# GpSimd copies the mixed queries of every level for the tiled products, and discarded results are stored in 8 bits

## The chip, the cores and the metric

One core of one Trainium2 chip runs the kernel. The metric is the device time of one execution in microseconds (us). TensorE (PE, with its weight loads shown as PEld), VectorE (DVE), ScalarE (ACT), GpSimd (POOL) and SyncE (SP, which issues the DMAs) each work through their own instruction stream in order, and wait for each other by semaphores.

## The reference

One layer over 2048 latent tokens and 256 context tokens of width 1024, all float32. What matters here is the gated linear recurrence of 8 heads with head width 128, run forwards and backwards:

```
q, i, zf, zb = four projections of h          # per head: (tokens, 128)
f = lb + (1 - lb) * sigmoid(z);  k = 1 - f    # one f and one k for each direction
S_t = diag(f_t) S_{t-1} + k_t v_t^T           # a 128 x 128 state
o_t = S_t^T q_t                               # the two directions are added
```

Beside it stand a gated short convolution, an input projection and an output projection, and RMS norms.

## The kernel before, in words

Large projections. All projections are products of f16 high and low parts, three matmuls for each piece (lines 963 to 965), arranged as seven products of half-size blocks instead of eight. They fill TensorE nearly throughout. The 32 scan segments (8 heads times 4 groups of 512 tokens) are threaded between them: `merge_steps` and `run` emit the steps of a segment's chain (`scan_steps`, with the weights of the table `PACE`) between the matmuls of the next projection. A scheduler then sets each engine's final order.

A segment's chain. Inside a segment the products of the recurrence are built up by levels 0 to 6, where level `lev` joins blocks of B = 2^lev tokens. `K` and `Q` (`s.qf`) hold keys and queries of both directions side by side, 2 x 512 columns. At each level DVE multiplies half of the keys by a decay (`level_k`, line 509) and half of the queries (`level_q`, line 516), in place. For a level, the half of the tokens that takes the forward copy and the half that takes the backward copy are interleaved in runs of B; `mix` is the access pattern that walks them so.

Tiled products. `levels(lev)`, called for levels 0, 2 and 4, issues two sets of sixteen 32 x 32 products (line 656). The trace has two records for each float32 matmul, so one set is 32 records. The first set (`i` = 0) uses the tiles that were kept: `ks` and `q` for level 0, `km` and `qm` of level 1 or 3 later. The second set (`i` = 1) uses `km` of the level itself, copied by ACT into one piece (`mixed`, line 626), and the queries, read through `mix` out of `Q`. `held(lev)`, for levels 1, 3 and 5, has GpSimd copy the mixed queries into the tile `qm` (line 633, one buffer) before `level_q` overwrites `Q`. `level6` uses `qm` of level 5 (line 675), then `K` and `Q` directly (line 682).

So within a segment the order on the queries is: `Q` made (line 592), second set of level 0, `level_q(0)`, copy `qm1`, `level_q(1)`, sets of level 2, `level_q(2)`, copy `qm3`, `level_q(3)`, sets of level 4, `level_q(4)`, copy `qm5`, `level_q(5)`, products of `level6`.

Other users of GpSimd are the casts of the input norm in the first windows (line 325) and four copies of 32 x 128 elements into `A` in each segment (line 690). `junk` (line 149) receives results that nobody reads: squares and absolute values of which only the accumulated sum is used (lines 280, 433, 812, 1051, 1621, all on ACT).

Of the kernel before, what the change touches and what calls it, by code (L numbers as in the profile page):

```python
# [9 lines left out]
F32 = mybir.dt.float32  # L10
F16 = mybir.dt.float16
# [3 lines left out]
U8 = mybir.dt.uint8  # L15
# [5 lines left out]
P = 128  # L21
D = 1024
# [4 lines left out]
GW = 512  # L27
# [11 lines left out]
NSUB = 5  # L39
SB = 32  # L40
# [17 lines left out]
def sub(t, off, dims):  # L58
    return bass.AP(t.tensor, t.offset + off, [list(t.ap[0])] + [list(d) for d in dims])
# [3 lines left out]
def hybrid_layer(ctx: ExitStack, tc, x, cx, w_ada, b_ada, w_in, w_out, fnorm_w, small_d, masks, ident_d, sel_d, out):  # L63
    nc = tc.nc
    V, S, G, PE, SY = nc.vector, nc.scalar, nc.gpsimd, nc.tensor, nc.sync

    cp = ctx.enter_context(tc.tile_pool(name="cp", bufs=1))
# [4 lines left out]
    scp = scg.__enter__()  # L72
# [23 lines left out]
    def pa_t(nm):  # L96
        return pa.tile([P, 512], F32, tag="pa", name=nm)
# [48 lines left out]
        return hp.tile([P, HK, 2, HW], F16, tag="hop", name=nm)  # L146

    hc = scp.tile([P, 3, 2, HK, CTX], F16, name="hc", bufs=1)
    junk = cp.tile([P, D], F16, name="junk")

    def rsqrt(ss, n, inv_n, nm):
        v = sp.tile([P, 16], F32, tag="rs_v", name=f"rsv_{nm}", bufs=2)[:, :n]
# [348 lines left out]
    def mix(t, n, B, np_, off=0):  # L501
        return sub(t, off, [[2 * B, np_], [n + B, 2], [1, B]])
# [28 lines left out]
    class Seg:  # L531
# [85 lines left out]
        def begin_levels(s):  # L617
            s.start_levels()
            s.mixed(0)

        def mixed(s, lev):

            B = 1 << lev
            n = s.n
            s.km = scp.tile([P, GW], F32, tag="km", name=f"km{lev}_{s.nm}", bufs=3)
            S.activation(sub(s.km, 0, [[2 * B, n // (2 * B)], [B, 2], [1, B]]), mix(s.K, n, B, n // (2 * B)), AF.Copy)  # L626

        def held(s, lev):

            B = 1 << lev  # L630
            n = s.n
            qm = scp.tile([P, GW], F32, tag="qm", name=f"qm{lev}_{s.nm}", bufs=1)
            G.tensor_copy(sub(qm, 0, [[2 * B, n // (2 * B)], [B, 2], [1, B]]), mix(s.qf, n, B, n // (2 * B)))  # L633
            s.kept = s.km, qm
            s.update(lev)

        def update(s, lev):
            n = s.n
            level_k(s.K, s.cur, n, lev)
            if lev < NSUB:  # L640
                s.mixed(lev + 1)
            level_q(s.qf, s.cur, n, lev)
            s.cur, s.off = level_tot(s.cur, s.tot, s.tot7, n, lev, s.off)

        def levels(s, lev):

            n = s.n
            B = 1 << lev
            k1, q1 = s.kept if lev else (s.ks, s.q)
            pt = pa_t(f"A{lev}_{s.nm}")  # L650
            for i in range(2):
                for ch in range(NCH):
                    for j in range(P // SB):
                        o = ch * P + j * SB
                        c = i * P + ch * SB
                        PE.matmul(pt[j * SB:(j + 1) * SB, c:c + SB], (s.km if i else k1)[:, o:o + SB],  # L656
                                  mix(s.qf, n, B, SB // (2 * B), o) if i else q1[:, o:o + SB], start=True, stop=True)
            s.update(lev)
            at = [pt[:, i * P:(i + 1) * P].rearrange("p (c t) -> p c t", c=NCH) for i in range(2)]
            if lev == 0:  # L660
                s.Ac = scp.tile([P, NCH, SB], F32, tag="Ac", name=f"Ac_{s.nm}")
                S.activation(s.Ac, at[0], AF.Copy)
            for i in range(2) if lev else (1,):
                V.copy_predicated(s.Ac, sub(mask, (lev - 1 + i) * SB, [[0, NCH], [1, SB]]), at[i])
# [566 lines left out]
    for hd in range(HEADS):  # L1231
# [4 lines left out]
        for i, g in enumerate(order(h.prim, NG)):  # L1236
            s = Seg(hd, g * GW, GW, 0, f"{hd}_{g}")
# [23 lines left out]
    for wi, (kind, a, i) in enumerate(stretch):  # L1261
# [37 lines left out]
        if wi > 0 and stretch[wi - 1][0] == "head":  # L1299
            _, pa_h, pi = stretch[wi - 1]  # L1300
# [30 lines left out]
        if kind == "head" and a >= 6:  # L1331
            n = (a - 6) * NG + i
            extra += [paced(0.2, lambda k=k: wo_scan(k)) for k in (2 * n, 2 * n + 1)]
        if kind == "pair":
            n = (a - 1) * 2 + i
# [383 lines left out]
```

## Time and profile before

| what | value |
|---|---|
| time, median of 3 runs | 2145.19 us (2144.64 to 2151.95) |
| time of the profiled execution | 2148.78 us |
| span of its instructions | 2147.0 us |
| TensorE matmul busy | 2065.5 us |
| DVE, ACT, POOL busy | 1648.6, 1203.0, 193.8 us |
| scan stage (100 to 1262 us of the span) | 1162 us |

A row of a group shows line, engine, operation, tiles written and read, shapes and the count; behind the bar stand busy time in us and the mean duration of one in ns; behind the second bar the idle time of the engine just before these instructions, and what ended it. A row of the timeline shows start and duration in us; merged rows have a count. A matmul's end is modelled, so the weight loads (PEld) show TensorE's pace more sharply.

### The profile page before, as it was taken

What the parts mean: (1) busy time and instruction counts of PE and PEld (TensorE: products, weight loads), DVE (VectorE), ACT (ScalarE), POOL (GpSimd) and SP (SyncE); (2) the same over time, 40 slices, a digit from 0 to 9 for tenths busy, and PEclk for the clock granted to TensorE, in tenths of its full rate; (3) what the DMA queues carried; (4) which work ended last, traced back from release to release, by engine and by line L of the source; (5) the groups of instructions that cost most, each with busy time, mean ns of one, the idle gap of its engine ahead of it and who ended that gap; (6) DMA issues with size and microseconds to landing.
All of it is one profiled execution on the core that took longest, in us unless ns stands there. A gap on an engine that the chain in (4) does not pass through costs nothing. (4 is left out here: it accounts for less than half of the span.)

```text
span 2147.0 us, 53020 instructions
## 1 busy us (share of the span) xinstructions
PE 2065.5 (96%) x22011; PEld 1455.3 (68%) x22011; DVE 1648.6 (77%) x3413; ACT 1203.0 (56%) x2406; POOL 193.8 (9%) x272
## 2 busy tenths in 40 slices
PE   5988999999999999999999999999999999999998
PEld 2877878888888888888888887444444444444443
DVE  6787988878778787788787877687778655687775
ACT  7965666767567666676776655345444423333332
POOL 0121111111111111111111100000000000000000
PEclk8999999999999999999999999999999999999999
DMA  9567533452445343544654568833443105542421
GB/s 357 192 209 265 180 120 128 146 173 86 135 137 159 116 133 119 180 114 153 193 168 131 152 198 254 255 125 101 138 138 99 62 28 189 198 144 89 136 80 59
DMA packets 239398, 324.12 MB, mean 151 GB/s; under 512 B 66611, under 2 KB 168371, under 8 KB 237365
## 3 DMA queue, kind: packets, MB, share of 16 engines
q1 hardware_dynamic: 236996, 316.80, 47.0%
q8 instruction: 172, 2.82, 0.5%
q10 hardware_dynamic: 2160, 3.93, 0.5%
q14 instruction: 70, 0.57, 0.1%
HBM read 240.19 MB, written 67.37 MB: 143 GB/s over the span
## 5 line engine op out<-in xcount | busy, mean ns | idle before, releaser
L964 PEld LDWEIGHTS <-e_p 128*128 128x128 f16 x1332 | 130.4, 98 | 68.7 <-issue 19.0
L509 DVE TENSOR_TENSOR K<-K,tot 128x512 f32<-128x512 f32 x192 | 135.6, 706 | 42.8 <-ACT km L626 25.9
L626 ACT ACTIVATE km<-K 128x512 f32<-128x512 f32 x192 | 129.2, 674 | 69.7 <-DVE K L509 65.5
L963 PEld LDWEIGHTS <-e_p 128*128 128x128 f16 x1332 | 130.4, 98 | 53.2 <-issue 1.4
L965 PEld LDWEIGHTS <-e_p 128*128 128x128 f16 x1332 | 130.4, 98 | 52.0 <-issue 0.9
L516 DVE TENSOR_TENSOR Q<-Q,tot 128x512 f32<-128x512 f32 x192 | 132.9, 692 | 26.5 <-PE A L656 15.1
L633 POOL COPY qm<-Q 128x512 f32<-128x512 f32 x96 | 80.7, 840 | 781.6 <-DVE Q L516 781.6
L964 PEld LDWEIGHTS <-whib_p 128*128 128x128 f16 x888 | 87.0, 98 | 38.6 <-issue 5.2
L963 PEld LDWEIGHTS <-whib_p 128*128 128x128 f16 x888 | 86.9, 98 | 37.2 <-issue 0.8
L963 PEld LDWEIGHTS <-whia_p 128*128 128x128 f16 x888 | 86.9, 98 | 35.9 <-DMA hop3B<-Hd3B 2.4
L965 PEld LDWEIGHTS <-wloa_p 128*128 128x128 f16 x888 | 86.8, 98 | 35.1 <-issue 1.3
L965 PEld LDWEIGHTS <-wlob_p 128*128 128x128 f16 x888 | 86.9, 98 | 34.4
L964 PEld LDWEIGHTS <-whia_p 128*128 128x128 f16 x888 | 86.9, 98 | 33.4 <-issue 1.3
L181 ACT ACTIVATE e_p<-ws_p,sc_p 128x512 f16<-128x512 f32 x108 | 77.2, 718 | 56.9 <-DVE ws_p L468 40.0
L690 POOL COPY A<-Ac 32x128 f32<-32x128 f32 x128 | 79.5, 621 | 132.9 <-ACT A L686 103.8
L886 ACT ACTIVATE cv<-c,small 128x512 f32<-128x512 f32 (+1 forms) x36 | 24.3, 674 | 112.5 <-DVE c L904 63.3
L970 ACT ACTIVATE u<-sa,sx_w 128x256 f32<-128x256 f32 (+1 forms) x111 | 58.1, 523 | 47.0 <-PE sa L965 38.2
L1630 POOL TENSOR_TENSOR x_o<-x_o,fw 128x512 f32<-128x512 f32 x1 | 1.3, 1266 | 871.0 <-ACT junk L1621 871.0
L182 DVE SCALAR_TENSOR_TENSOR e_p<-ws_p,sc_p,e_p 128x512 f16<-128x512 f32 x108 | 79.4, 747 | 0.0
L433 ACT ACTIVATE junk<-ws_p 128x1024 f16<-128x1024 f32 x72 | 75.6, 1050 | 5.1 <-DMA ws_p<-in_w_in 4.9
L181 ACT ACTIVATE hiS_o<-y_o,sc_y 128x1024 f16<-128x1024 f32 x32 | 36.7, 1148 | 72.9 <-PE sa_o L964 32.1
L970 ACT ACTIVATE p<-sa,sx_w 128x256 f32<-128x256 f32 (+1 forms) x111 | 57.4, 517 | 24.1 <-PE sa L965 24.1
(863 smaller groups left out, 7044.8 us busy)
## 6 DMA issues: line engine op xcount, KB each, us to landing
ws_p<-in_w_in SPq DMA_DIRECT2D x72, 512.0 KB, 4.4
y_o<-yT SPq DMA_DIRECT2D x32, 512.0 KB, 4.2
xt_x<-in_x SPq DMA_DIRECT2D x16, 512.0 KB, 6.0
wa<-in_w_ada SPq DMA_DIRECT2D x16, 512.0 KB, 10.1
Gd<-zs SPq DMA_DIRECT2D x32, 256.0 KB, 2.9
sg<-Gd SPq DMA_DIRECT2D x32, 256.0 KB, 3.7
yT<-y SPq DMA_DIRECT2D x32, 256.0 KB, 2.4
wos<-in_w_out SPq DMA_DIRECT2D x32, 256.0 KB, 3.3
```

What stands on the lines that cost most here:

```text
L181: S.activation(hi, src, AF.Copy, scale=st[:, 0:1])
L182: V.scalar_tensor_tensor(lo, src, st[:, 0:1], hi, ALU.mult, ALU.subtract)
L433: S.activation(junk.rearrange("p (k n) -> p k n", k=KT), stage[i], AF.Abs, accum_out=r)
L509: V.tensor_tensor(m, m, sub(cur, nb + 1, [[2, np_], [-(nb + 1), 2], [0, B]]), ALU.mult)
L516: V.tensor_tensor(m, m, sub(cur, 1, [[2, np_], [nb - 1, 2], [0, B]]), ALU.mult)
L626: S.activation(sub(s.km, 0, [[2 * B, n // (2 * B)], [B, 2], [1, B]]), mix(s.K, n, B, n // (2 * B)), AF.Copy)
L633: G.tensor_copy(sub(qm, 0, [[2 * B, n // (2 * B)], [B, 2], [1, B]]), mix(s.qf, n, B, n // (2 * B)))
L690: G.tensor_copy(A3[js, :, js], s.Ac[js])
L963: PE.matmul(ps, hi[:, k], rh, start=start and k == 0, stop=False, skip_group_check=not start)
L964: PE.matmul(ps, hi[:, k], right(name, 1, k), start=False, stop=False, skip_group_check=not start)
L965: PE.matmul(ps, lo[:, k], rh, start=False, stop=k == nk - 1, skip_group_check=not start)
L970: last_keep.append(S.activation(r, ps, AF.Copy, scale=sx))
```

## The change

There is a new function `queries(lev)`: it takes a tile `qm` and lets GpSimd copy the mixed queries of that level into it. It is called for level 0 at the end of `begin_levels`, for levels 1, 3 and 5 where the copy stood already, and for levels 2 and 4 at the end of `held`. The second set of `levels` reads that tile. `qm` has two buffers instead of one. `junk` is kept in 8 bits instead of 16; its size falls from 2 KB to 1 KB of each partition.

```
-    junk = cp.tile([P, D], F16, name="junk")
+    junk = cp.tile([P, D], U8, name="junk")
...
         def begin_levels(s):
             s.start_levels()
             s.mixed(0)
+            s.q2 = s.queries(0)
...
-        def held(s, lev):
+        def queries(s, lev):
...
-            qm = scp.tile([P, GW], F32, tag="qm", name=f"qm{lev}_{s.nm}", bufs=1)
+            qm = scp.tile([P, GW], F32, tag="qm", name=f"qm{lev}_{s.nm}", bufs=2)
             G.tensor_copy(sub(qm, 0, [[2 * B, n // (2 * B)], [B, 2], [1, B]]), mix(s.qf, n, B, n // (2 * B)))
-            s.kept = s.km, qm
+            return qm
+
+        def held(s, lev):
...
+            s.kept = s.km, s.queries(lev)
             s.update(lev)
+            if lev + 1 < NSUB:
+                s.q2 = s.queries(lev + 1)
...
                         PE.matmul(pt[j * SB:(j + 1) * SB, c:c + SB], (s.km if i else k1)[:, o:o + SB],
-                                  mix(s.qf, n, B, SB // (2 * B), o) if i else q1[:, o:o + SB], start=True, stop=True)
+                                  (s.q2 if i else q1)[:, o:o + SB], start=True, stop=True)
```

A segment now has six copies on GpSimd instead of three, 192 in the whole kernel instead of 96. With two buffers, the copy for level 2 takes the buffer of level 0 and waits for the second set of level 0; the copy for level 3 takes that of level 1 and waits for the first set of level 2, and so on. `level_q` of levels 0, 2 and 4 now waits for a copy on GpSimd, where it waited for a set on TensorE.

Two places show what the scheduler makes of it. Lines of the changed kernel below the edit are 9 higher (line 656 is 665, 866 is 875, 963 is 972). On DVE, in head 4 and token group 3, this stands before (`Q` with `f` is `level_q(0)`, `Q` with `tot` the next level, the other rows belong to weights, gates and the mask of level 0):

```order
L465 TENSOR_TENSOR ws_p_12842<-s_p_12917,ws_p_12842 128x512
L516 TENSOR_TENSOR Q_3_12747<-Q_3_12747,f_3_12269 128x256x2
L827 TENSOR_TENSOR zs_3_12944<-z_3_12717,zs_3_12944 128x512
L664 COPY_PREDICATED Ac_3_13009<-mask,A_4_3_12971 128x128
L182 SCALAR_TENSOR_TENSOR wlob_p_12915<-ws_p_12844,sc_p_12908,whib_p_12914 128x512
L516 TENSOR_TENSOR Q_3_12747<-Q_3_12747,tot_3_12964 128x128x2x2
```

and this stands now, 27 rows earlier, right behind the row that makes `Q`:

```order
L592 TENSOR_TENSOR Q_3_12861<-q_3_12604,f_3_12377 128x1024
L522 TENSOR_TENSOR tot_3_13078<-f_3_12377 128x512
L516 TENSOR_TENSOR Q_3_12861<-Q_3_12861,f_3_12377 128x256x2
L875 SCALAR_TENSOR_TENSOR y_2_12896<-oT_2_12891,small,sg_2_12730 128x512
L509 TENSOR_TENSOR K_3_12378<-K_3_12378,tot_3_13078 128x128x2x2
L794 TENSOR_REDUCE ymax<-y_2_12896 128x1
L516 TENSOR_TENSOR Q_3_12861<-Q_3_12861,tot_3_13078 128x128x2x2
```

`level_q` of levels 0 and 1 moved ahead of the segment's first set on TensorE; the other rows kept their order but for a place or two.

On TensorE, in head 2 and token group 2, the second set of level 0 stands here before, inside the last products of `sb`:

```order
L964 LDWEIGHTS whib_p_5276
L964 MATMUL sb_7464<-hop11T_6979,whib_p_5276 128x256
L656 MATMUL A_2_2_7483<-Q_2_7458,km_2_2_7478 32x32 x16
L965 LDWEIGHTS wlob_p_5277
L965 MATMUL sb_7464<-hop11T_6979,wlob_p_5277 128x256
L963 LDWEIGHTS e_p_5278
L963 MATMUL sa_7430<-hop11T_7229,e_p_5278 128x256
```

and here now, behind the first four products of the next group (`sa` with `e_p`):

```order
L974 LDWEIGHTS wlob_p_5319
L974 MATMUL sb_7524<-hop11T_7033,wlob_p_5319 128x256
L972 LDWEIGHTS e_p_5320
L972 MATMUL sa_7490<-hop11T_7289,e_p_5320 128x256
L973 LDWEIGHTS e_p_5320
L973 MATMUL sa_7490<-hop11T_7289,e_p_5320 128x256
L974 LDWEIGHTS e_p_5320
L974 MATMUL sa_7490<-hop11T_7289,e_p_5320 128x256
L972 LDWEIGHTS e_p_5320
L972 MATMUL sa_7490<-hop11T_7289,e_p_5320 128x256
L665 MATMUL A_2_2_7545<-qm_2_2_7540,km_2_2_7538 32x32 x16
```

It moved past five matmuls. In most other segments the sets keep their place among the matmuls.

More of the change, by code (lines that the diff above doesn't have):

```diff
@@ L626, in mixed @@
             S.activation(sub(s.km, 0, [[2 * B, n // (2 * B)], [B, 2], [1, B]]), mix(s.K, n, B, n // (2 * B)), AF.Copy)
+        def queries(s, lev):
+            B = 1 << lev
+            n = s.n
+            qm = scp.tile([P, GW], F32, tag="qm", name=f"qm{lev}_{s.nm}", bufs=2)
+            G.tensor_copy(sub(qm, 0, [[2 * B, n // (2 * B)], [B, 2], [1, B]]), mix(s.qf, n, B, n // (2 * B)))
+            return qm
         def held(s, lev):
@@ L631, in held @@
             n = s.n
-            qm = scp.tile([P, GW], F32, tag="qm", name=f"qm{lev}_{s.nm}", bufs=1)
-            G.tensor_copy(sub(qm, 0, [[2 * B, n // (2 * B)], [B, 2], [1, B]]), mix(s.qf, n, B, n // (2 * B)))
-            s.kept = s.km, qm
+            s.kept = s.km, s.queries(lev)
             s.update(lev)
+            if lev + 1 < NSUB:
+                s.q2 = s.queries(lev + 1)
         def update(s, lev):
```

## The prediction

> **What bounds the kernel now.** I read the page's busy shares first, then the busy times of the scan stage (100 to 1262 us), the only stage that the change touches apart from `junk`.
>
> ```profile
> PE 2065.5 (96%) x22011; PEld 1455.3 (68%) x22011; DVE 1648.6 (77%) x3413; ACT 1203.0 (56%) x2406; POOL 193.8 (9%) x272
> 100.00:1262.00 1162.00, 1120.09 (x17150) 980.69 (x17151) 949.46 (x2089) 773.46 (x1695) 176.03 (x246) 1.00 0.50 153
> ```
>
> TensorE is the bound: in the scan stage it is busy 1120.1 of 1162 us at the full granted clock (1.00), so at most 42 us of it are open idle time, while DVE has 1162 - 949.5 = 213 us, ACT 389 and GpSimd 986. Only two things can therefore shorten the run: less TensorE time for the same products, or fewer of those 42 us. Next I took the groups of the tiled products by form, then the timeline around single sets.
>
> ```profile
> L656 PE MATMUL A<-Q,km 128*32 128x32 f32 x3072 | 48.9, 204 | 3.2 <-DVE Q L516 1.4 <-ACT km L626 0.5 <-DVE Q L592 0.4
> L656 PE MATMUL A<-qm,km 128*32 128x32 f32 x2048 | 29.6, 199 | 4.7 <-POOL qm L633 4.6
> L656 PEld LDWEIGHTS A<-Q,km 128*32 128x32 f32 x3072 | 39.5, 111 | 7.3 <-DVE Q L592 3.1 <-DVE Q L516 1.9 <-ACT km L626 0.9
> L656 PEld LDWEIGHTS A<-qm,km 128*32 128x32 f32 x2048 | 22.4, 112 | 18.7 <-issue 11.8 <-POOL qm L633 6.8
> L675 PE MATMUL A<-qm,km 128*32 128x64 f32 x1024 | 21.3, 222 | 2.1 <-POOL qm L633 1.4 <-ACT km L626 0.6
> L675 PEld LDWEIGHTS A<-qm,km 128*32 128x32 f32 x1024 | 16.0, 109 | 9.2 <-issue 6.5 <-POOL qm L633 2.6
> L682 PE MATMUL A<-Q,K 128*32 128x64 f32 x1024 | 20.3, 219 | 1.5 <-DVE Q L516 1.5
> L682 PEld LDWEIGHTS A<-Q,K 128*32 128x32 f32 x1024 | 16.5, 110 | 2.5 <-DVE Q L516 2.3 <-issue 0.2
> ```
>
> A second set (queries read through `mix` out of `Q`) is busy 48.9 / 96 = 0.509 us, a first set with a copied tile 29.6 / 64 = 0.463 us. TensorE's open waits for the query chain are 4.6 + 1.4 + 1.5 + 1.4 = 8.9 us on PE, and 6.8 + 2.6 + 2.3 + 1.9 = 13.6 us if the weight loads' idle time is counted, part of which lies under running matmuls.
>
> **Term A, the products read one piece.** By the rows above the 96 second sets would save between 96 x (0.509 - 0.463) = 4.4 us (PE) and 39.5 - 96 x 22.4 / 64 = 5.9 us (PEld). But they differ in more than the pattern: they also follow straight behind another set. The timeline separates some of it (head 4, token group 0, levels 0 and 2, then a level-2 set that had waited):
>
> ```profile
> 708.63 0.35 PEld L656 LDWEIGHTS A<-q,ks 128*32 128x32 f32 x32 [0.21 <-issue]
> 708.88 0.45 PEld L656 LDWEIGHTS A<-Q,km 128*32 128x32 f32 x32
> 713.75 0.35 PEld L656 LDWEIGHTS A<-qm,km 128*32 128x32 f32 x32 [0.21 <-issue]
> 714.00 0.41 PEld L656 LDWEIGHTS A<-Q,km 128*32 128x32 f32 x32
> 598.92 0.35 PEld L656 LDWEIGHTS A<-Q,km 128*32 128x32 f32 x32
> ```
>
> Level 0 (runs of one element) takes 0.45 us, level 2 (runs of 4) 0.41, but a level-2 set that stood ready in the queue ran in 0.35 with the same pattern. So for levels 2 and 4 the pattern may cost nothing where the set stands ready. The lower bound is level 0 alone by a set that also had waited (the row at 481.08 below, 0.40): 32 x 0.05 = 1.6 us; the upper bound is 5.9. I take the PE groups' 4.4, since both level kinds show some excess in nearly all sets that did not wait. The Trainium skill (SBUF — State Buffer, section "Door 1: The DMA port swizzle", its remark on cachelines) says that a read pays when it leaves a 16-byte line, so that four float32 in a row are free; by that only level 0 would gain and the term would be about 1.6 us. The 0.35 row agrees with it, the 0.41 row does not.
>
> **Term B, waits that go.** The chain between the sets of level 0 and level 2 in that segment:
>
> ```profile
> 709.50 1.12 DVE L516 TENSOR_TENSOR Q<-Q,f 128x512 f32<-128x512 f32 x1 [0.96 <-PE A L656]
> 710.75 0.81 POOL L633 COPY qm<-Q 128x512 f32<-128x512 f32 x1 [26.10 <-DVE Q L516]
> 711.60 0.69 DVE L516 TENSOR_TENSOR Q<-Q,tot 128x512 f32<-128x512 f32 x1
> ```
>
> Before, all of it (1.12 + 0.81 + 0.69) starts when the level-0 sets end. After, `level_q(0)`, copy 1 and `level_q(1)` run ahead of those sets, and only the copy for level 2 stays between: about 1.8 us shorter, so the waits ahead of level 2 go. Between levels 2 and 4, `level_q(2)` leaves the chain and the copy for level 4 enters it, 0.69 against about 0.84 us: no gain. Ahead of `level6`, `level_q(4)` leaves it and nothing enters: 0.69 us and the second set's 0.25 shorter. The longest such waits are 0.48 and 0.88 us:
>
> ```profile
> 1039.60 0.54 PEld L675 LDWEIGHTS A<-qm,km 128*32 128x32 f32 x32 [0.48 <-POOL qm L633]
> 1041.02 0.49 PEld L682 LDWEIGHTS A<-Q,K 128*32 128x32 f32 x32 [0.88 <-DVE Q L516]
> ```
>
> So of the 8.9 us I count the 1.4 and 1.5 ahead of `level6`, the 1.4 on `level_q`, and a quarter of the 4.6 on `qm` (level 2's share as against level 4's, my estimate): 5.5 us. Bounds: 0 and 13.6.
>
> **Term C, the new copy in front of level 0.** Where `Q` is made long before its set, the copy is hidden by that distance. In eight places TensorE already waits for `Q` itself (from the list of what the sets of line 656 waited for, then one of them, head 2, token group 2):
>
> ```profile
>   DVE Q L592: 3.5, 8
> 479.80 1.23 DVE L592 TENSOR_TENSOR Q<-q,f 128x1024 f32<-128x1024 f32 x1 [1.05 <-ACT q L600]
> 480.57 0.27 PE L963 MATMUL sb<-hop11T,whib_p 128*128 128x256 f16 x1
> 480.68 0.27 PE L964 MATMUL sb<-hop11T,whib_p 128*128 128x256 f16 x1
> 481.08 0.40 PEld L656 LDWEIGHTS A<-Q,km 128*32 128x32 f32 x32 [0.41 <-DVE Q L592]
> L633 POOL COPY qm<-Q x96: 604/654/2340, 107.4 to 1251.6; 128x512 f32<-128x512 f32 x96
> ```
>
> `Q` is ready at 481.03. The copy (0.61 us at least, 0.65 at the median, level 0's pattern not shown) makes it 481.7 or 481.8 with the passing on. The set stands five matmuls later now, 5 x 0.11 = 0.55 us, so TensorE would reach it near 481.5. The wait grows from about 0.1 to 0.3 us: 8 x 0.2 = 1.6 us lost. Bounds: 0, and 8 x 0.7 = 5.6 us with a copy as long as 1.17 us, which the trace shows where a copy meets DVE:
>
> ```profile
> 283.86 1.17 POOL L633 COPY qm<-Q 128x512 f32<-128x512 f32 x1 [4.12 <-DVE Q L516]
> 283.86 0.69 DVE L509 TENSOR_TENSOR K<-K,tot 128x512 f32<-128x512 f32 x1
> 382.83 0.61 POOL L633 COPY qm<-Q 128x512 f32<-128x512 f32 x1 [4.17 <-DVE Q L516]
> 383.11 0.88 DVE L509 TENSOR_TENSOR K<-K,tot 128x512 f32<-128x512 f32 x1 [0.19 <-ACT km L626]
> ```
>
> **Off the path.** DVE stops waiting for TensorE at `level_q` and waits for GpSimd instead:
>
> ```profile
> DVE Q L516 <- PE A L656: 32.1, 43, 1.5
> DVE Q L516 <- POOL qm L633: 10.9, 29, 0.6
> ```
>
> The 32.1 us fall away for DVE, whose 213 us of idle time hide it: no gain, and a cover for what the copies cost it. GpSimd's 96 more copies of 0.84 us mean are 81 us of its 986 idle. In the first windows casts of the norm (line 325) queue behind a copy that may wait for TensorE, and behind them the stores and loads of a token group:
>
> ```profile
> L633 POOL COPY qm<-Q 128x512 f32<-128x512 f32 x96 | 80.7, 840 | 781.6 <-DVE Q L516 781.6
> PE sa L963 <- DMA hop3B<-Hd3B: 2.2, 1, 2.2
> ```
>
> TensorE waited for such a load once, 2.2 us. I cost the casts at nothing, with 2 us as the bound.
>
> Results in 8 bits: no row shows ACT writing 8 bits. Its squares and sums into 16 bits are the nearest:
>
> ```profile
> L433 ACT ACTIVATE junk<-ws_p 128x1024 f16<-128x1024 f32 x72 | 75.6, 1050 | 5.1 <-DMA ws_p<-in_w_in 4.9
> L626 ACT ACTIVATE km<-K 128x512 f32<-128x512 f32 x192 | 129.2, 674 | 69.7 <-DVE K L509 65.5 <-DVE rsa_o L159 2.2 <-DVE tot L522 1.2
> ```
>
> 512 elements into float32 take 674 ns and 1024 into f16 1050, so time follows elements and not bytes. I take 0; 10% either way would be 105 ns for one of them, under ACT's 389 us of idle time.
>
> **Sum.** -4.4 (A) - 5.5 (B) + 1.6 (C) = -8.3 us. The profiled execution took 2148.78 us (span 2147.0), which becomes 2140.5. It lies 3.6 us above the median of the runs, 2145.19, which becomes 2136.9; that is the forecast, -0.4%. A measurement of this kernel can tell about 0.5%, 10.7 us, from no change: faster means under 2134.5, slower over 2155.9.
>
> **Rivals.** Larger gain: all waits for the query chain go at the weight loads' price (13.6), the sets save 5.9 and term C is hidden by the moved sets: -19.5, 2125.7 us. For it speaks that each set removed from a chain also frees the weight loads; against it that half of the waits on `qm` are ahead of level 4, where the chain stays as long.
>
> Nothing: the second sets are slow since they follow another set, not by their pattern (the 0.35 row at 598.92), and waits only change place. Then A is 1.6, B 2.9 (`level6`), C 1.6 to 5.6: between -2.9 and +1.1, about 2144.
>
> Slower: DVE becomes what TensorE waits for. A copy of 0.61 us lengthens a DVE instruction on two SBUF tiles (0.88 against 0.69 above), and `level_q` now stands right behind the row that starts the copy, so DVE waits in place, with evacuations of product banks (line 974) queued behind it. If TensorE inherits 0.21 us for each of the 96 new copies, the 20 us eat the gain of 9.9 and more; that is the point from which it is slower by over 0.5%, and the whole 0.61 would give +48.7, 2194 us. Against it: DVE's 213 us, and its 29 present waits for a copy come to 10.9 us. The Trainium skill (SBUF — State Buffer, section "Who interferes with whom") has VectorE with two SBUF inputs and a reading GpSimd instruction block each other for a whole instruction. By that every collision costs one side up to 0.61 us; the trace shows GpSimd losing more (1.17) than DVE (0.19).
>
> **Chances.** Forecast 0.45, larger gain 0.3, nothing 0.18, slower 0.07. Faster by over 0.5%: the larger gain's 0.3 and 0.04 of the forecast's upper side, 0.34. Slower: 0.06. Within: 0.60. The range goes down to the larger gain's price and up to the upper end of the case "nothing" with the 2 us of the casts (2145.2 + 1.1 + 2): 2125 to 2149. Left out are the slower case and about 0.1 for a gain beyond that price.
>
> **What would show it.** Right: PEld of the second sets at 0.35 to 0.38 us in the mean, waits for line 634 in front of levels 2 and 6 gone, some 0.3 us at each of eight level-0 sets. Wrong: second sets still at 0.41 (A), TensorE waits for `qm` of over 10 us (B, C), or DVE's wait for GpSimd past 60 us together with new waits of line 972 for DVE (slower). Matmul records that stay the same while the span falls by more than 10 us would mean I missed the cause.

## The result, and the profile after

The changed kernel takes 2178.1 us (median of 4 runs, 2176.51 to 2180.52), the kernel before beside it 2146.82 (4 runs). The ratio is 1.0143, 95% interval 1.013 to 1.0156: 31 us slower, where 8 us faster was forecast and 2149 was the upper end of the range. In the changed kernel the lines of `levels` and later are 9 higher (656 is 665, 970 is 979), and the copy of line 633 is line 634.

The page's busy shares and the scan stage of the changed kernel, which now ends about 28 us later:

```profile
PE 2064.4 (95%) x22011; PEld 1452.8 (67%) x22011; DVE 1660.4 (76%) x3413; ACT 1209.3 (56%) x2406; POOL 276.7 (13%) x368
100.00:1290.00 1190.00, 1119.84 (x17127) 977.53 (x17126) 957.57 (x2082) 778.94 (x1697) 258.01 (x341) 1.00 0.49 149
```

TensorE has the same work as before in the stage (1119.8 against 1120.1 us) at the same clock (1.00); its idle time there went from 42 to 70 us. All of the loss is waiting. What TensorE waited for, first in the kernel before (rows the prediction did not show), then in the changed one; behind the colon stand us in total, times, longest:

```profile
PE sa L963 <- ACT u L970: 7.5, 12, 1.1
PE sb L963 <- DVE f L974: 2.9, 2, 1.7
PE T_c L706 <- ACT kT_c L699: 1.6, 5, 0.4
```

```profile
PE sa L972 <- ACT u L979: 19.1, 24, 1.3
PE A L665 <- POOL qm L634: 9.7, 12, 2.3
PE oT L873 <- ACT kT L708: 6.4, 4, 1.6
PE T_c L715 <- ACT kT_c L708: 6.2, 8, 1.4
PE sb L972 <- DVE f L983: 4.9, 4, 1.5
```

These five grew by 29.7 us together (before, `A` for `qm` was 4.6, and `oT` for `kT` was not there). Only 5.1 of that are the tiled products waiting for a copy. The rest stands in front of other products. The large projections wait for a PSUM bank (where a product lies until it is copied out, or evacuated), which ScalarE (`sa` for `u`) or VectorE (`sb` for `f`) empties late. The context chain waits for its transposed keys (`T_c` for `kT_c`), and the output's transposes (`oT`) for a bank of the pool `px` out of which ScalarE copies `kT`.

What VectorE waits for, what ScalarE's copies `km` wait for, and the rows of the copies and of a result in 8 bits, in the changed kernel:

```profile
DVE Q L516 <- POOL qm L634: 29.6, 45, 1.0
ACT km L627 <- DVE K L509: 93.3, 63, 3.4
```

```profile
L634 POOL COPY qm<-Q 128x512 f32<-128x512 f32 x192 | 163.4, 851 | 721.4 <-PE A L665 350.7 <-DVE Q L516 142.9 <-DVE Q L592 88.2
L433 ACT ACTIVATE junk<-ws_p 128x1024 uint8<-128x1024 f32 x72 | 75.7, 1052 | 5.4 <-DMA ws_p<-in_w_in 5.1
```

`level_q` no longer waits for TensorE (32.1 us before) but 29.6 us for its copy (10.9 before). ScalarE's copies wait 27.8 us more for K (65.5 before). The tiled products did get a little shorter: the time in which any of them ran fell from 78.9 to 75.9 us. The copies have the mean length that was assumed (851 ns against 840), and the 8-bit results cost nothing (1052 ns against 1050).

One segment shows how a query update reaches a projection. In the changed kernel, head 4, token group 0 (start and duration in us; in brackets the idle time before and its releaser):

```profile
708.44 3.55 POOL L634 COPY qm<-Q 128x512 f32<-128x512 f32 x1 [9.31 <-DVE Q L592]
711.23 0.91 DVE L811 SCALAR_TENSOR_TENSOR Z<-Z,tot,Ts 128x128 f32<-128x128 f32 x1
712.06 1.09 DVE L516 TENSOR_TENSOR Q<-Q,f 128x512 f32<-128x512 f32 x1
713.57 0.75 DVE L811 SCALAR_TENSOR_TENSOR Z<-Z,tot,Ts 128x128 f32<-128x128 f32 x1
716.21 0.68 DVE L509 TENSOR_TENSOR K<-K,tot 128x512 f32<-128x512 f32 x1
716.92 0.63 ACT L627 ACTIVATE km<-K 128x512 f32<-128x512 f32 x1 [3.05 <-DVE K L509]
717.46 0.46 ACT L979 ACTIVATE u<-sa,sx_w 128x256 f32<-128x256 f32 x1
717.97 0.27 PE L972 MATMUL sa<-hop17T,e_p 128*128 128x256 f16 x1 [1.09 <-ACT u L979]
```

The same places in the kernel before:

```profile
700.65 0.63 ACT L626 ACTIVATE km<-K 128x512 f32<-128x512 f32 x1 [1.25 <-DVE K L509]
701.19 0.46 ACT L970 ACTIVATE u<-sa,sx_w 128x256 f32<-128x256 f32 x1
706.64 0.35 DVE L729 SCALAR_TENSOR_TENSOR s_c<-s_c,tot_c,T_c 128x128 f32<-128x128 f32 x1 [2.15 <-ACT s_c L728]
709.50 1.12 DVE L516 TENSOR_TENSOR Q<-Q,f 128x512 f32<-128x512 f32 x1 [0.96 <-PE A L656]
```

Before, `level_q(0)` ran some 8 us behind this place, after gaps of 2.15 and 0.96 us in VectorE's row. Now it stands ahead of K's update; ScalarE waits 3.05 us for K in place of 1.25, the evacuation of `sa` stands behind that in ScalarE's row, and TensorE waits 1.09 us for the bank. About half of the 1.8 us is `level_q(0)` itself. The other half is two updates of `Z` that met a GpSimd copy (0.91 and 0.75 us, where the same update takes 0.34 at 714.78); the first of these copies itself took 3.55 us. VectorE had 213 us of idle time in the stage before, but in this stretch (699.9 to 721.5 us) it has none.

### The profile page after: what moved, and what is told of

Same layout as the page of the kernel before. It is cut to its first block, busy times and chain, and to the rows that moved or that the text cites. A ratio compares the mean times of both kernels' runs of the same rounds, so it can differ in the third digit from the quotient of the medians.

```text
span 2174.7 us, 53188 instructions
## 1 busy us (share of the span) xinstructions
PE 2064.4 (95%) x22011; PEld 1452.8 (67%) x22011; DVE 1660.4 (76%) x3413; ACT 1209.3 (56%) x2406; POOL 276.7 (13%) x368
## 4 chain that ended last, share of the span: by engine, by line
PE 57%; DVE 23%; ACT 9%; DMA 5%; issue 4%; POOL 2%; SPq 0%; POOLq 0%; ACTq 0%; DVEq 0%
PE sa L972 7%; PE sa L973 7%; PE sa L974 7%; PE sb L972 3%; PE sb L974 3%; PE sb L973 3%; DVE K L509 3%; PE sa_o L972 2%; DVE Q L516 2%; PE sa_o L973 2%; PE sa_o L974 2%; DVE e_p L182 2%; PE sc L974 2%; PE sc L973 2%; PE sc L972 2%
## 5 line engine op out<-in xcount | busy, mean ns | idle before, releaser
L634 POOL COPY qm<-Q 128x512 f32<-128x512 f32 x192 | 163.4, 851 | 721.4 <-PE A L665 350.7
L433 ACT ACTIVATE junk<-ws_p 128x1024 uint8<-128x1024 f32 x72 | 75.7, 1052 | 5.4 <-DMA ws_p<-in_w_in 5.1
L979 ACT ACTIVATE p<-sb,sx_w 128x256 f32<-128x256 f32 (+1 forms) x111 | 58.0, 522 | 32.2 <-PE sb L974 29.1
L181 ACT ACTIVATE hiS_o<-y_o,sc_y 128x1024 f16<-128x1024 f32 x32 | 36.8, 1152 | 69.7 <-PE sa_o L973 32.1
```

What stands on the lines that cost most here:

```text
L181: S.activation(hi, src, AF.Copy, scale=st[:, 0:1])
L433: S.activation(junk.rearrange("p (k n) -> p k n", k=KT), stage[i], AF.Abs, accum_out=r)
L979: last_keep.append(S.activation(r, ps, AF.Copy, scale=sx))
```

## The experiments

I had two theories. **Order:** the freed `level_q` runs early on VectorE, delays K's updates, with them ScalarE's `km` copies and the evacuations behind these. **Copies:** 96 more GpSimd copies cost by themselves, by meeting VectorE's instructions and by standing on the way from Q to the products. "Pinned" below means that a set's last product reads Q through the strided view again, so that `level_q` has to wait for the set; where all copied levels are pinned (e1, e5, e10), 3 to 8 of VectorE's 3413 rows stand in another order than before in the traces, against at least 414 in the changed kernel. What some of the expectations call contention is tested here as traffic on the memory that both engines use; no run shows anything on shared issue slots. "Us over before" is (ratio - 1) x 2146.

| run | order of `level_q` | new copies | ratio, 95% interval | us over before |
|---|---|---|---|---|
| changed kernel | free | 96 | 1.0143, 1.013 to 1.0156 | 31 |
| e1 | pinned | 96 | 1.0127, 1.0105 to 1.0149 | 27 |
| e2 | as before | 96, read by nobody | 1.0042, 1.003 to 1.0055 | 9 |
| e3 | free | 0 | 1.0041, 1.0027 to 1.0054 | 9 |
| e4 | as before | 0, 8-bit results | 1.0, 0.9988 to 1.0011 | 0 |
| e5 | pinned | 0 | 1.0006, 0.9997 to 1.0015 | 1 |
| e6 | free | 96, of km, read by nobody | 1.0189, 1.0174 to 1.0204 | 41 |
| e7 | levels 2, 4 free | 64 | 1.0087, 1.0072 to 1.0102 | 19 |
| e8 | level 0 free | 32 | 1.0119, 1.01 to 1.0138 | 26 |
| e9 | level 0 free | 0 | 1.0027, 1.0018 to 1.0037 | 6 |
| e10 | level 0 pinned | 32 | 1.0066, 1.0051 to 1.0081 | 14 |
| e11 | level 0 behind K's next update | 32 | 1.0083, 1.0068 to 1.0098 | 18 |
| e12 | levels 2, 4 free | 0 | 1.0033, 1.0021 to 1.0046 | 7 |
| e13 | free | 96, not read by the sets | 1.0248, 1.0233 to 1.0263 | 53 |
| e14 | level 0 pinned, 2, 4 free | 96 | 1.0144, 1.0127 to 1.0161 | 31 |

**e1: order of before, all copies.**

```
-  (s.q2 if i else q1)[:, o:o + SB]
+  (mix(s.qf, ...) if (ch, j) == (NCH - 1, P // SB - 1) else s.q2[:, o:o + SB]) if i else q1[:, o:o + SB]
```

> The changed kernel, but the last product of each second set (levels 0, 2 and 4) reads Q again through the strided view; so VectorE's update of Q (level_q) must wait for that set as in the kernel before, and VectorE's row of instructions is again that of before. All 192 copies and 31 of 32 one-piece products stay. Order theory (the early level_q delays K's update, ScalarE's km copy, the evacuation behind it and so TensorE): the loss goes, 2137 to 2150 us, that is 4 to 10 us under before or level with it. Contention theory (96 more GpSimd copies share SBUF and issue slots with VectorE): the copies are all there, so 2165 us or more.

2173.91 us against 2146.38. The order theory falls as the main cause: with the order of before, 27 of the 31 us stay. But the wait has moved. What TensorE waited for:

```profile
PE A L665 <- POOL qm L634: 26.6, 29, 2.9
PE sa L973 <- ACT u L980: 10.3, 15, 1.2
PE T_c L716 <- ACT kT_c L709: 2.4, 5, 0.6
```

`sa` for `u` and `T_c` for `kT_c` are nearly back, `oT` for `kT` is gone, and the sets wait 26.6 us for their copies, 22 more than before.

**e2: traffic alone.** The kernel before with 8-bit results and two buffers of `qm`, plus

```
+  t = scp.tile([P, GW], F32, tag="qm", name=f"qd{lev}_{s.nm}", bufs=2)
+  G.tensor_copy(t, s.km)
```

> The kernel before with 96 further GpSimd copies of km, one ahead of each even level, into a second qm buffer that nothing reads; junk in 8 bits; VectorE's and ScalarE's rows of instructions are those of before, word for word. Order theory: 2143 to 2152 us (before, or 5 us over it). Contention theory: most of the 31 us, 2165 to 2180 us.

2155.26 us, 9 over before: between the theories. Query updates of this run, then one meeting (GpSimd's copy and VectorE's `level_q(1)`, which takes 0.69 undisturbed):

```profile
L516 DVE TENSOR_TENSOR Q<-Q,tot 128x512 f32<-128x512 f32 x192 | 151.2, 787 | 19.5 <-PE A L663 11.6 <-POOL qm L638 7.7
```

```profile
717.91 0.60 POOL L624 COPY qd<-km 128x512 f32<-128x512 f32 x1
717.99 1.07 DVE L516 TENSOR_TENSOR Q<-Q,tot 128x512 f32<-128x512 f32 x1
```

The copy that began first ran at full speed, and VectorE's instruction became 0.38 us longer. The kernel before has 692 ns in the place of 787: 192 x 0.095 = 18 us more of VectorE's time, 0.19 for each added copy. With the smaller rises of other rows VectorE is busy 25 us longer than before (1674.0 against 1648.6), of which 9 us reach the end. So traffic has a price even where nobody waits for a copy.

**e3 and e5: no copies, order free and pinned.**

```
-  s.q2 = s.queries(0)        # and s.queries(lev + 1)
+  s.q2 = qz                  # a standing tile of zeros, one buffer of qm; e5 with e1's pin as well
```

> The changed kernel without its 96 new copies: the second sets of levels 0, 2 and 4 multiply with a standing tile of zeros in place of the mixed queries (this part of the computation is left out), so level_q waits for nothing on TensorE and runs early, as in the changed kernel or earlier. Order theory: the loss stays without a copy, 2165 to 2190 us. Contention theory: the loss goes with the copies, and only the one-piece reads are left, 2135 to 2147 us.

> The changed kernel without its 96 copies (the second sets of levels 0, 2 and 4 multiply with a standing tile of zeros, which leaves this part of the computation out), but with the last product of each of these sets reading Q through the strided view, so that level_q waits for the set and VectorE's row of instructions is that of before. Left are the one-piece reads alone. The step of the prediction that gave them 4.4 us: 2141 to 2143 us. If what the pinned and the free kernel lose is not order, this one loses too: 2150 us or more.

e3 takes 2155.67 us against 2146.38, and e5 2148.03 against 2146.21. Without a copy the free order still costs 9 us, although it has the one-piece reads; the pinned one costs nothing that can be told. Neither time lies in a range that was expected. So order has a price of its own, 9 us beside the 31 of the whole, and it is paid at places seen in the changed kernel. TensorE's waits in e3:

```profile
PE sa L974 <- ACT u L981: 12.7, 24, 1.3
PE oT L875 <- ACT kT L710: 6.4, 4, 1.6
```

e5 leaves little of the price of the reads: with the strided last product its tiled products were only 1.5 us shorter in TensorE's records than those of before (77.4 against 78.9), not 4.4. The rows of e9 and e12 show why, under term A below.

**e4: results in 8 bits alone.** The kernel before with

```
-    junk = cp.tile([P, D], F16, name="junk")
+    junk = cp.tile([P, D], U8, name="junk")
```

> The kernel before with junk in 8 bits and nothing else. Order and contention theories alike: the time of before, 2145 to 2148 us. If the 8-bit write itself costs (its producers seen 2 ns longer each), at most 1 us more.

2145.80 us against 2146.38: no effect.

**e6: free order, with traffic nobody waits for.** e2's copies, and in the second sets

```
-  (s.q2 if i else q1)[:, o:o + SB]
+  ident[:, 0:SB] if i else q1[:, o:o + SB]
```

> The changed kernel with its second sets of levels 0, 2 and 4 reading a standing tile (this part of the computation is left out) and with the 96 new copies turned into copies of km that nobody waits for: the early order of level_q and the GpSimd traffic together, without the handing over from VectorE through GpSimd to TensorE. If the two costs just add (9 us of order over before, 9 of traffic): 2162 to 2168 us, and the rest of the loss is the wait for the copies. If traffic and order make each other worse: 2172 to 2182 us, and the handing over costs nothing in the early order.

2186.58 us. This run says little: GpSimd's spare copies waited 445 us for the `km` of the next level, and the copies that are needed stood behind them.

**e7 and e8: copies by level.** e7 drops the copy of level 0, e8 those of levels 2 and 4; the levels without a copy read the strided view. e7, then e8:

```
-            s.q2 = s.queries(0)
```

```
-            if lev + 1 < NSUB:
-                s.q2 = s.queries(lev + 1)
```

> The changed kernel without the copy of level 0 (its second set reads the strided view as before, and level_q(0) waits for it again); levels 2 and 4 as changed. If each copied level costs its share: 2146 + 21 = 2167 us. If the loss sits in level_q(0) being early and in the late copies of level 0: 2146 to 2153 us.

> The changed kernel with the copy of level 0 alone; levels 2 and 4 read the strided view as before. If each copied level costs its share: 2146 + 10 = 2156 us. If the loss sits in level 0: 2165 to 2178 us.

2164.26 and 2170.49 us against 2146.21: e7 lies near the 2167 of each copied level paying its share, e8 inside the range of a loss that sits in level 0, so the two do not agree on where it sits. The two losses (19 and 26) make 45, more than the 31 of both together: neither part keeps its price when the other is there. Each has its own signature, first e7's, then e8's waits of TensorE:

```profile
PE A L664 <- POOL qm L633: 18.2, 21, 2.3
PE oT L873 <- ACT kT L708: 6.4, 4, 1.6
```

```profile
PE sa L971 <- ACT u L978: 18.4, 25, 1.3
PE T_c L714 <- ACT kT_c L707: 5.8, 8, 1.4
```

**e9, e10 and e12: level 0 and levels 2 and 4 taken apart.** e9 and e12 are e8 and e7 with the tile of zeros in place of the copies, e10 is e8 pinned. e9, e12 and the pin of e10:

```
-            s.q2 = s.queries(0)
+            s.q2 = qz
```

```
-                s.q2 = s.queries(lev + 1)
+                s.q2 = qz
```

```
-  (mix(s.qf, ...) if lev else s.q2[:, o:o + SB])
+  (mix(s.qf, ...) if lev or (ch, j) == (NCH - 1, P // SB - 1) else s.q2[:, o:o + SB])
```

> The kernel before (with 8-bit junk), but the second set of level 0 multiplies with a standing tile of zeros (this part of the computation is left out), so that level_q(0) waits for nothing; no copy is added; levels 2 and 4 as before. Early level_q(0) by itself delays the evacuations: 2152 to 2158 us, with TensorE's waits for evacuated products (sa for u) above 11 us against 7.5 before. If the 24 us that the kernel with level 0's copies alone lost is the copies' traffic and not the order: 2143 to 2149 us.

> The kernel with the 32 copies of level 0 alone, but its last product reads Q through the strided view, so that level_q(0) waits for the set again and VectorE's row is that of before. Order of level_q(0) the larger part: 2148 to 2155 us, and the wait of T_c for kT_c back near 1.6 us, sa for u near 8. If it is the copies in whatever order: 2165 us or more, as with the free order (2170.5).

> As the run on level 0 without copies, for levels 2 and 4: their second sets multiply with zeros (left out of the computation), level 0 as before; no copy is added. If the 18 us of the kernel with the copies of levels 2 and 4 are mostly the sets' wait for the copies (13.6 us more of A for qm) and the rest order (oT for kT, 6.4 us): 2149 to 2154 us, with oT for kT still near 6.4 us. If they are order: 2160 us or more.

2151.82, 2160.60 and 2154.41 us against 2145.59. For level 0 the free order alone costs 6 us (2151.82, just under the 2152 expected at least), the 32 copies alone 14 (between the two expectations), and both 26. For levels 2 and 4 the free order alone costs 7 of the 19 (2154.41, just over the 2154 expected at most, with `oT` for `kT` at 6.4 as expected). TensorE's waits, of e9, e10 and e12:

```profile
PE sa L972 <- ACT u L979: 14.7, 25, 1.5
PE T_c L715 <- ACT kT_c L708: 4.8, 5, 1.4
```

```profile
PE sa L971 <- ACT u L978: 8.6, 15, 1.2
PE A L663 <- POOL qm L634: 7.5, 12, 1.5
```

```profile
PE oT L874 <- ACT kT L709: 6.4, 4, 1.6
```

`sa` for `u` and `T_c` for `kT_c` come with a free `level_q(0)`, `oT` for `kT` with free updates of levels 2 and 4, copies or not; waits for `qm` come with the copies.

**e11: level_q(0) behind K's next update.** e8, with `level_q(0)` taken out of `update(0)` and written into `held(1)`, where an edge keeps it behind the last VectorE instruction written (`level_k(1)`):

```
+            level_k(s.K, s.cur, n, 1)
+            s.mixed(2)
+            with tc.issue_after(last):
+                level_q(s.qf, s.cur0, n, 0)
+            s.kept = km, s.queries(1)
+            level_q(s.qf, s.cur, n, 1)
```

> The kernel with the 32 copies of level 0 alone and free, but with level_q(0) written behind level_k(1) and held there, so that K's next update runs ahead of it on VectorE; the copies of levels 0 and 1 come as the row then gives. If level_q(0) ahead of K's updates is the cause of its 24 us: 2146 to 2155 us, and sa for u near 8 us. If the loss is the traffic, or Q's chain being later costs as much: 2162 us or more, with the waits of the sets (A) for qm or Q up.

2163.91 us against 2145.59. Held back by one step, level 0's loss falls from 26 to 18, not to the 9 or less that the order theory gave. `T_c` still waits 5.0 us for `kT_c` and `sa` 12.5 for `u`: in the segment shown above `level_q(0)` and `level_q(1)` still stand among the context chain's updates.

**e13: the sets no longer wait for copies.** The changed kernel with

```
-  (s.q2 if i else q1)[:, o:o + SB]
+  ident[:, 0:SB] if i else q1[:, o:o + SB]
```

> The changed kernel with all its copies of Q, for which level_q still waits, but its second sets of levels 0, 2 and 4 multiply with a standing tile in place of the copies (this part of the computation is left out), so that no set waits for a copy. Parts that add: order 9 us, traffic 9 us, so 2162 to 2167 us, and the sets' wait for copies is the rest of the 31. If traffic and early order make each other worse by themselves (level_q held by its copy, K's updates behind it): 2172 to 2180 us, with sa for u near 19 us, as in the changed kernel.

2198.74 us against 2145.34: 22 us slower than the changed kernel, though a wait was taken away, and beyond what either view expected. VectorE's waits, then TensorE's:

```profile
DVE K L509 <- ACT km L627: 41.1, 48, 2.8
DVE Q L516 <- POOL qm L634: 30.8, 49, 1.0
```

```profile
PE sa L972 <- ACT u L979: 27.9, 26, 1.8
PE sb L972 <- DVE f L983: 11.2, 11, 1.3
```

e3 had the same freedom without the copies and lost 9 us. Only `level_q` still needs the new copies themselves. It waits for its copy in VectorE's row with the evacuation `f` (line 983) behind it; `sb` waits 11.2 us for `f`, against 4.5 in e3. The copies of levels 1, 3 and 5 also stand behind the new ones in GpSimd's row. Part of the difference may be VectorE's row of instructions itself: at least 260 of its rows stand in another order in e13 than in e3.

**e14: level_q(0) pinned, all copies.** The pin of e1 for level 0 alone:

```
-  (s.q2 if i else q1)[:, o:o + SB]
+  (mix(s.qf, ...) if (lev, ch, j) == (0, NCH - 1, P // SB - 1) else s.q2[:, o:o + SB]) if i else q1[:, o:o + SB]
```

> The changed kernel with all its copies, but the last product of level 0's second set reads Q through the strided view, so that only level_q(0) waits for its set again; levels 2 and 4 are free. If the parts add by levels (14 us for level 0 pinned with its copies, 18 for levels 2 and 4): 2176 to 2180 us, no better than the changed kernel. If the early level_q(0) is what the changed kernel pays beyond the copies: 2165 to 2170 us, with sa for u near 8 us and T_c for kT_c near 2 us.

2175.49 us against 2145.34, the same loss as the changed kernel. The parts add (14 for e10 and 19 for e7 make 33). TensorE's waits:

```profile
PE A L665 <- POOL qm L634: 25.6, 28, 2.9
PE sa L973 <- ACT u L980: 8.0, 14, 1.1
```

Against the changed kernel `sa` for `u` fell by 11.1 us, `T_c` for `kT_c` by 3.8, and `A` for `qm` rose by 15.9: what is saved in one place comes back in the other.

No run was faster than the kernel before, and none points to a version that would be: without copies and in the old order (e5) there is nothing to gain that can be told.

## Why the prediction was wrong

**The failed step: "Off the path".** It said of VectorE's waits that its "213 us of idle time hide it: no gain, and a cover for what the copies cost it". That cover is a sum over a stage; in the stretch shown, where a segment begins, VectorE has no gap, and the gaps that `level_q(0)` used before lie behind it. Three prices were put at nothing there. Traffic: 9 us alone (e2). Order: 9 us alone (e3). Copies on the way of an engine that works in order: with the order of before the sets wait for them (22 us more, e1), with the free order VectorE does, 29.6 us with evacuations behind it. These do not simply add: copies cost 27 us in the old order and 22 more than the order's 9 in the new one.

**Term A** was too large, and its reason failed: "both level kinds show some excess" is so, but only level 0's comes from the pattern. In e9 the second sets of level 0 read one piece (`qz`) and those of levels 2 and 4 the strided view; in e12 it is the other way round. Weight loads of e9, then of e12, then a level-0 second set and a whole level 2 (two sets in one row) of the changed kernel:

```profile
L665 PEld LDWEIGHTS A<-qz,km 128*32 128x32 f32 x1024 | 13.0, 108 | 0.0
L665 PEld LDWEIGHTS A<-Q,km 128*32 128x32 f32 x2048 | 25.8, 108 | 4.3 <-ACT km L629 2.8 <-ACT junk L821 0.9 <-issue 0.4
L666 PEld LDWEIGHTS A<-Q,km 128*32 128x32 f32 x1024 | 14.2, 113 | 3.1 <-DVE Q L594 3.1
L666 PEld LDWEIGHTS A<-qz,km 128*32 128x32 f32 x2048 | 25.9, 108 | 1.7 <-ACT km L628 1.4 <-issue 0.2
529.14 0.41 PEld L665 LDWEIGHTS A<-qm,km 128*32 128x32 f32 x32
534.99 0.65 PEld L665 LDWEIGHTS A<-qm,km 128*32 128x32 f32 x64 [0.21 <-issue]
```

A level-0 second set takes 13.0 / 32 = 0.41 us in one piece and 14.2 / 32 = 0.44 through the view, so 32 of them save 1.2 us (2.1 in TensorE's own records, 17.8 against 15.7). A second set of levels 2 and 4 takes 25.9 / 64 = 0.40 us in one piece and 25.8 / 64 = 0.40 through the view: nothing is saved. The changed kernel agrees: 0.41 at level 0 for the 0.45 of before, and 0.65 us for both sets of level 2, where the rows at 713.75 and 714.00 of the kernel before span 0.66. What is left of those sets' excess over the 0.35 of a first set is that they follow another set, as the rival "nothing" said; its 1.6 us was the size to take. The time in which any of these products ran fell by 3.0 us in the changed kernel; what the rest of that is, and whether any of it shortens the run, is not shown.

**Term B** said that waits of 5.5 us go. `level_q` is indeed free of TensorE, and the waits of the sets for Q (1.4 us) are gone. But ahead of `level6` most of the 2.9 us counted there stayed, 0.8 and 1.8 us in place of 1.4 and 1.5:

```profile
PE A L684 <- POOL qm L634: 0.8, 1, 0.8
PE A L691 <- DVE Q L516: 1.8, 3, 1.1
```

What was not asked is what the freed instruction displaces: VectorE's row is full there, so K's updates come later. Its sign was wrong: the same freedom cost 9 us in e3, with the shorter products already in it.

**Term C** counted 0.2 us at each of eight late sets of level 0. In the changed kernel, head 2, token group 2 (the place that the prediction worked out):

```profile
490.55 0.82 POOL L634 COPY qm<-Q 128x512 f32<-128x512 f32 x1 [12.21 <-PE sb L974]
491.43 0.35 PEld L665 LDWEIGHTS A<-qm,km 128*32 128x32 f32 x32 [0.84 <-POOL qm L634]
```

The copy of level 0 took 0.82 us here (3.55 in the segment above), not 0.61 to 0.65; 0.82 is the shortest of the 32 copies of level 0, and their median is 0.99. Second sets of level 0 waited eight times for a copy, 4.7 us together, where they had waited 0.4 for Q; all waits of the sets for copies grew by 5.1 us instead of 1.6, inside the bound of 5.6. The mechanism was right and the size too small; with the order of before (e1) it would have been 22, since then levels 2 and 4 wait too. The step that saw "no gain" between levels 2 and 4 missed that.

**The rival "slower"** had the place nearly right and a chance of 0.07. VectorE does wait in place for copies (29.6 us), and 31 us / 96 copies = 0.32 us lies beyond its deciding point of 0.21. But the evacuations that came late are mostly ScalarE's (TensorE waits 11.6 us more for `u`), which in the segment shown stand behind a `km` that waits for K, and less VectorE's own (2.0 us more for `f`). Against it the prediction set that "the trace shows GpSimd losing more (1.17) than DVE (0.19)". That was read from two meetings; in e2 VectorE lost 0.38 in one, and on the average 0.19 for every copy. The Trainium skill (SBUF — State Buffer, section "Who interferes with whom") has the port pair that VectorE and GpSimd share as an exclusive lock; e2's pair of rows, where the later starter is the one that is lengthened, agrees with that.

**Right** was that results in 8 bits cost nothing (e4). The casts, put at nothing with a bound of 2 us, stayed inside it: TensorE's wait for the load of `hop3B` went from 2.2 to 3.6 us, and is 3.6 in e3 without the copies too. Of the prediction's own signs of being wrong two came: second sets still at 0.41 us, and waits of TensorE for `qm` over 10 us (9.7 and 0.8). The third, VectorE's wait for GpSimd past 60 us, was set too high by a factor of two.

Open is why e13 loses 22 us more than the changed kernel, and how much of the changed kernel's 31 us is traffic rather than waiting in place: the two were only separated in the order of before (9 of 27). The copies lengthen VectorE's instructions less in the changed kernel: it is busy 12 us longer than before (1660.4 against 1648.6), in e1 28 us and in e2 25. Copies by another engine than GpSimd were not tried.

## What to carry to other kernels

Idle time summed over a stage is no cover: look at the stretch where the new wait or the freed instruction will stand, and ask what is in that row behind it. Taking a wait away from an engine that works in order also moves its work forward, ahead of something; when the thing displaced feeds an evacuation, the bound engine pays. A sum over rows can mislead as well: a set that follows another is charged for it, whatever it reads, so change the pattern alone before pricing it (e9, e12). To find which of order and traffic costs, pin the order with a small dependency and keep the copies (e1), or keep the order and add copies that nobody reads (e2), and read which wait takes the place of which.

## What the runs showed of the hardware

A GpSimd copy of 128 x 512 float32 that nobody waits for lengthened VectorE's query updates (two SBUF tiles) by 0.19 us on the average (e2: 787 ns against 692 over 192 of them, with 96 copies), and by 0.38 us in the meeting shown. The reverse is larger at its worst: the level-0 copy at 708.44 took 3.55 us, where the one at 490.55 took 0.82. A copy of the same size that gathers single elements (level 0) took 0.82 us at least, one in longer runs (levels 3 to 5) 0.61.

A set of sixteen 32 x 32 float32 products that follows another set took 0.40 to 0.41 us of weight loads whether it read its 32 columns in one piece or in runs of 4 or 16 elements, and 0.44 to 0.45 in single elements (e9 and e12).
